# One flag on a hybrid diffusion kernel: the instruction queues ordered by the framework's second model

## Chip, core and metric

The kernel runs on one core of a Trainium2 chip. The metric is the device time of one execution in microseconds (us), lower is better. TensorE (PE) does the matmuls, VectorE (DVE) and GpSimd (POOL) the elementwise work, ScalarE (ACT) the casts and activations, SyncE (SP) issues the DMAs. Each engine works through its own queue of instructions in the order in which they stand there, and waits at an instruction until what it needs is ready.

## The reference, cut to what matters

Two layers work on 256 latent tokens and 256 context tokens of width 1024. Each layer mixes tokens with three branches (windowed GQA with a sink, multi-head latent attention, and a chunked bidirectional gated linear attention, GLA), merges them with sigmoid gates, projects, and then runs a gated FFN with a width-3 convolution.

```python
proj = (rmsnorm(x) * (1 + scale) + shift) @ w_in       # one combined projection
ya = window_gqa(q_a, k_a, v_a, ctx, sink)              # softmax attention
yb = mla(q_b, kv_b)                                    # softmax attention, low-rank q and kv
yc = gla(q_c, k_c, v_c, gates)                         # softplus gates, a scan per direction, chunks
m  = sum(sigmoid(proj_gate[b]) * (y[b] @ w_br[b]) for b in branches)
x  = x + gate1 * (m @ w_out)
u  = conv3(rmsnorm_mod(x) @ w_up) ; x = x + gate2 * (silu_gate(u) @ w_down)
```

Layer 0 needs all 512 tokens. Layer 1 puts out only the 256 latent ones. The last step is an RMS norm of the latent stream.

## The kernel before

All tensors lie transposed, 128 channels on the partitions and tokens along the row; `KT` is 8, for 1024 channels. Products are made in three parts so that they come out at nearly float32: a weight tile is loaded by SP (`raw`, L161), cast on ACT to `whi` (L164), and the rest `wlo = raw - whi` is made on DVE or POOL (L168). A `unit` (L176 on) is one output tile of 128 channels: 24 matmuls, for each of 8 channel blocks k the three products `whi` x `hh` (L172), `whi` x `hl` (L173) and `wlo` x `hh` (L174). It goes to one PSUM bank.

Each layer runs these stages in time:

- win7 (L381 to L400): the first seven output tiles, k by k. In layer 0 the modulation of channel block k+1 is worked out here too: `mods_sum` (L359) and `mods_turn` (L369) on PE, then scale and shift on ACT, then `hh`, `hl` of that block. The norms use a sum over channels (L233), a chain of ten small DVE instructions for the reciprocal root (L197 to L239), and a matmul that spreads it over the partitions (L242); DVE and ACT then make `ht`, `hh`, `hl` (L265 to L267). Layer 1 takes two passes, context and latent, so it has two norms there.
- GLA (L430 to L750): gates are `lab`, made on ACT as Exp (L546) and Ln (L549) with a table load between; DVE scans them to `bb` (L555, L557); DVE, POOL and ACT turn `bb` into factors (L593 to L601), and PE makes the products of pairs (L578). The value units (`cvr`, L473, with transposes to `cv`, L484) are work for PE that does not need the gates.
- Attention, twice four pairs of heads (L800 to L880): scores (L813, L817) to a PSUM tile, row maximum on DVE, Exp on ACT (L828) into a `p` buffer, a scale (L834), PE transposes (L850), `pth` on ACT (L854), `ptl` on DVE (L855), outputs (L866, L869). Units of the gates and branches stand between these as work for PE.
- Merge and w_out (L770 to L784, L1012 to L1029): `m` is summed over branches, `mh`, `ml` are made from it (L1012, L1013), then eight units of w_out. In layer 0 DVE also works through rows of the modulation product, `jk` (L104), one per loaded tile and stream.
- FFN (L1045 to L1146): norm, up units, convolution on ACT and DVE (L1088 to L1092), down units.

The program text is written in the order of the algorithm, with hand-made lists of work to fill in. What stands in each engine's queue is decided by the framework, which orders the instructions by a planner's model of the engines, on top of the dependences. Buffers of a pool are handed out in that order too. The context that does this is opened in one place, and it is the line that the change touches:

```python
    with tile.TileContext(nc) as tc:
        hybrid(nc, tc, aps, out)
```

## Time and profile before

| | |
|---|---|
| median of 3 runs | 1519.2 us (1518.48 to 1521.23) |
| profiled execution, its own time | 1519.25 us |
| its span, first to last instruction | 1517.5 us |
| PE busy | 1438.5 us, 95% |
| PE weight loads (PEld) busy | 1243.2 us, 82% |
| DVE busy | 1218.2 us, 80% |
| ACT, POOL busy | 811.7 us (53%), 494.6 us (33%) |
| DMA | 213.28 MB, mean 141 GB/s |
| mean granted TensorE clock | 0.981 |

The span is cut into stages below by the time at which they ran. Busy time of PE is the time in which a matmul is under way; matmuls overlap by pipelining, so the time from one start to the next is the better measure of what one costs. Idle time of PE is the stage's length less its busy time. The granted clock is 1.00 where TensorE runs at 2.4 GHz and 0.50 where it runs at 1.2 GHz.

### The profile page before, as it was taken

What the parts mean: (1) busy time and instruction counts of PE and PEld (TensorE: products, weight loads), DVE (VectorE), ACT (ScalarE), POOL (GpSimd) and SP (SyncE); (2) the same over time, 40 slices, a digit from 0 to 9 for tenths busy, and PEclk for the clock granted to TensorE, in tenths of its full rate; (3) what the DMA queues carried; (4) which work ended last, traced back from release to release, by engine and by line L of the source; (5) the groups of instructions that cost most, each with busy time, mean ns of one, the idle gap of its engine ahead of it and who ended that gap; (6) DMA issues with size and microseconds to landing.
All of it is one profiled execution on the core that took longest, in us unless ns stands there. A gap on an engine that the chain in (4) does not pass through costs nothing. (4 is left out here: it accounts for less than half of the span.)

```text
span 1517.5 us, 27758 instructions
## 1 busy us (share of the span) xinstructions
PE 1438.5 (95%) x10062; PEld 1243.2 (82%) x10062; DVE 1218.2 (80%) x2289; ACT 811.7 (53%) x1698; POOL 494.6 (33%) x407
## 2 busy tenths in 40 slices
PE   6988999999999899999999999988989899989997
PEld 4766867778788799788888889967878889989997
DVE  5688597786888979798877979978777886897886
ACT  4565355565653346534244235675466776665663
POOL 0065233233320001446544640034354443133231
PEclk9999999999999999999999999999999999999999
DMA  8411122222236575444645865532132235556553
GB/s 315 169 50 62 46 76 78 72 74 77 84 105 224 178 229 182 139 158 149 214 139 157 289 232 153 182 105 79 56 102 85 89 108 186 179 163 198 175 172 93
DMA packets 107432, 213.28 MB, mean 141 GB/s; under 512 B 12000, under 2 KB 21600, under 8 KB 106272
## 3 DMA queue, kind: packets, MB, share of 16 engines
q1 hardware_dynamic: 106608, 210.86, 42.6%
q8 instruction: 79, 1.29, 0.3%
q10 hardware_dynamic: 688, 0.66, 0.1%
q14 instruction: 57, 0.47, 0.1%
HBM read 210.42 MB, written 1.05 MB: 139 GB/s over the span
## 5 line engine op out<-in xcount | busy, mean ns | idle before, releaser
L168 POOL TENSOR_TENSOR wlo<-raw,whi 128x512 fp32r<-128x512 f32 (+1 forms) x270 | 373.8, 1390 | 711.5 <-ACT whi L164 464.0
L164 ACT CAST whi<-raw 128x512 fp32r<-128x512 f32 (+1 forms) x614 | 360.5, 597 | 320.0 <-PE ps_mm L173 136.4
L172 PE MATMUL ps_mm<-hh,whi 128*128 128x512 f32 (+1 forms) x808 | 298.3, 369 | 11.7 <-ACT cvr L473 8.5
L173 PE MATMUL ps_mm<-hl,whi 128*128 128x512 f32 (+1 forms) x808 | 292.7, 362 | 0.0
L174 PE MATMUL ps_mm<-hh,wlo 128*128 128x512 f32 (+1 forms) x808 | 292.4, 362 | 0.2 <-DVE wlo L168 0.2
L168 DVE TENSOR_TENSOR wlo<-raw,whi 128x512 fp32r<-128x512 f32 (+1 forms) x344 | 238.1, 703 | 44.0 <-ACT whi L164 39.3
L172 PEld LDWEIGHTS ps_mm<-hh,whi 128*128 128x128 f32 x808 | 155.4, 192 | 38.9 <-ACT cvr L473 8.7
L174 PEld LDWEIGHTS ps_mm<-hh,wlo 128*128 128x128 f32 x808 | 154.9, 192 | 26.0 <-DVE wlo L168 0.6
L173 PEld LDWEIGHTS ps_mm<-hl,whi 128*128 128x128 f32 x808 | 155.4, 192 | 23.8 <-issue 0.4
L104 DVE SCALAR_TENSOR_TENSOR jk<-wm,sil 128x1024 f32<-128x1024 f32 x112 | 172.8, 1543 | 1.5 <-DMA wm<-wmod 0.4
L172 PE MATMUL ps_pair<-hh,whi 128*128 128x512 f32 (+1 forms) x312 | 109.8, 353 | 2.0 <-DVE cy L1092 1.7
L174 PE MATMUL ps_pair<-hh,wlo 128*128 128x512 f32 (+1 forms) x312 | 109.0, 352 | 0.3 <-DVE wlo L168 0.2
L173 PE MATMUL ps_pair<-hl,whi 128*128 128x512 f32 (+1 forms) x312 | 109.2, 351 | 0.0
L854 ACT CAST pth<-ps_pair 128x512 fp32r<-128x512 f32 (+1 forms) x96 | 49.4, 515 | 38.7 <-PE ps_pair L850 26.9
L172 PEld LDWEIGHTS ps_pair<-hh,whi 128*128 128x128 f32 x312 | 58.5, 188 | 11.6 <-ACT whi L164 3.2
L174 PEld LDWEIGHTS ps_pair<-hh,wlo 128*128 128x128 f32 x312 | 58.4, 188 | 9.6 <-DVE wlo L168 0.7
L855 DVE TENSOR_TENSOR ptl<-ps_pair,pth 128x512 fp32r<-128x512 f32 (+1 forms) x96 | 57.4, 597 | 10.8 <-ACT pth L854 10.2
L173 PEld LDWEIGHTS ps_pair<-hl,whi 128*128 128x128 f32 x312 | 58.6, 188 | 8.7
L172 PE MATMUL ps_mm<-ach,whi 128*128 128x256 f32 (+1 forms) x200 | 63.7, 319 | 1.2 <-ACT ach L1125 0.7
L173 PE MATMUL ps_mm<-acl,whi 128*128 128x256 f32 (+1 forms) x200 | 63.5, 317 | 0.0
L174 PE MATMUL ps_mm<-ach,wlo 128*128 128x256 f32 (+1 forms) x200 | 63.4, 317 | 0.0
L174 PE MATMUL ps_mm<-mh,wlo 128*128 128x256 f32 x192 | 55.4, 289 | 4.7 <-DVE wlo L168 4.7
(673 smaller groups left out, 3582.2 us busy)
## 6 DMA issues: line engine op xcount, KB each, us to landing
raw<-wup SPq DMA_DIRECT2D x184, 256.0 KB, 3.0
raw<-win SPq DMA_DIRECT2D x182, 256.0 KB, 2.7
wm<-wmod SPq DMA_DIRECT2D x72, 512.0 KB, 3.9
raw<-wdn SPq DMA_DIRECT2D x88, 256.0 KB, 2.9
raw<-wbr SPq DMA_DIRECT2D x48, 256.0 KB, 2.6
raw<-wout SPq DMA_DIRECT2D x48, 256.0 KB, 3.0
wm<-wm SPq DMA_DIRECT2D x8, 1024.0 KB, 8.1
x<-xT SPq DMA_DIRECT2D x16, 256.0 KB, 4.8
```

The source lines that it names most:

```text
L104: V.scalar_tensor_tensor(out=jk, in0=wm, scalar=1.0, in1=sil[:, s], op0=ALU.mult, op1=ALU.mult, accum_out=MOD[l][:, s, t:t + 1])
L164: S.copy(hi[:, :ncols], raw[:, :ncols])
L168: e.tensor_tensor(out=lo[:, :ncols], in0=raw[:, :ncols], in1=hi[:, :ncols].bitcast(F32), op=ALU.subtract)
L172: mm(o, ah, bh, start=start, stop=False)
L173: mm(o, ah, bl, start=False, stop=False)
L174: mm(o, al, bh, start=False, stop=stop)
L854: S.copy(dh, tv)
L855: V.tensor_tensor(out=dl, in0=tv, in1=dh.bitcast(F32), op=ALU.subtract)
```

## The change

The context gets one keyword. The same instructions are issued with the same dependences; the framework orders them with its second model, which follows engines and queues in time.

```diff
-    with tile.TileContext(nc) as tc:
+    with tile.TileContext(nc, schedule_with_timeline_sim=True) as tc:
         hybrid(nc, tc, aps, out)
```

Each engine has as many instructions as before (PE 9060, DVE 2146, ACT 1606, POOL 405, SP 740), but many stand elsewhere: on PE by up to 125 places, on DVE up to 53, on ACT up to 29, on SP up to 19. By the time at which they ran before, PE's order is the same in the two FFNs (from 650 to 900 us, and from 1360 us on), and differs in the rest. Three places follow; the number ahead of a row is its place in the engine's queue.

The first is ACT in the GLA stage of layer 0. `lab` are the two gate tiles, `cvr` copies a value unit out of PSUM. Before:

```order
74 L543 ACTIVATE lab_709<-ps_pair_723,pp_65 128x512
75 L546 ACTIVATE lab_708<-lab_708 128x1024
76 L546 ACTIVATE lab_709<-lab_709 128x1024
77 L549 ACT_TABLE_LOAD
78 L549 ACTIVATE lab_708<-lab_708 128x1024
79 L549 ACTIVATE lab_709<-lab_709 128x1024
80 L465 ACT_TABLE_LOAD
81 L465 ACTIVATE thc_742<-ps_mm_83 128x512
82 L473 COPY cvr_745<-ps_mm_746 128x512
```

And with the change:

```order
73 L473 COPY cvr_745<-ps_mm_746 128x512
74 L543 ACTIVATE lab_709<-ps_pair_723,pp_65 128x512
75 L484 COPY cv_665<-ps_o_784 128x128
76 L543 ACTIVATE lab_708<-ps_pair_716,pp_65 128x512
77 L546 ACTIVATE lab_708<-lab_708 128x1024
78 L484 COPY cv_667<-ps_o_784 128x128
79 L164 CAST whi_1051<-raw_1049 128x512
80 L164 CAST whi_1069<-raw_1067 128x512
81 L473 COPY cvr_876<-ps_mm_877 128x512
82 L543 ACTIVATE lab_709<-ps_pair_723,pp_65 128x512
83 L465 ACTIVATE thc_742<-ps_mm_83 128x512
84 L546 ACTIVATE lab_709<-lab_709 128x1024
```

The copy `cvr_745` moved from behind the Exp, Ln and both table loads to ahead of them. The copy of the next value unit, `cvr_876`, and two casts now stand ahead of the second gate tile and of both Ln, which follow behind row 84. In layer 1 the same happens with `cvr_10658`.

The second is DVE at the end of the merge of layer 0. `ml` are the low parts of the merged rows, `wlo_5644` is the first `wlo` of w_out, whose unit is `ps_mm_5640`. Before:

```order
710 L784 TENSOR_TENSOR m7_2244<-m7_2244,gt_5561 128x512
711 L136 SCALAR_TENSOR_TENSOR ab0_69<-mod0_67,pp_65 128x8 x2
712 L138 COPY ab0_69<-mod0_67 128x8
713 L1013 SCALAR_TENSOR_TENSOR ml2_5617<-m2_2239,mh2_5616 128x512
714 L1013 SCALAR_TENSOR_TENSOR ml3_5621<-m3_2240,mh3_5620 128x512
715 L1013 SCALAR_TENSOR_TENSOR ml4_5625<-m4_2241,mh4_5624 128x512
716 L1013 SCALAR_TENSOR_TENSOR ml5_5629<-m5_2242,mh5_5628 128x512
717 L1013 SCALAR_TENSOR_TENSOR ml6_5633<-m6_2243,mh6_5632 128x512
718 L1013 SCALAR_TENSOR_TENSOR ml7_5637<-m7_2244,mh7_5636 128x512
719 L168 TENSOR_TENSOR wlo_5644<-raw_5641,whi_5643 128x512
```

And with the change:

```order
697 L782 SCALAR_TENSOR_TENSOR gt_5501<-gt_5501,ps_mm_5503 128x512
698 L168 TENSOR_TENSOR wlo_5644<-raw_5641,whi_5643 128x512
699 L104 SCALAR_TENSOR_TENSOR jk_5306,mod0_67<-wm_5302,sil_75 128x1024
700 L784 TENSOR_TENSOR m6_2243<-m6_2243,gt_5501 128x512
701 L168 TENSOR_TENSOR wlo_5662<-raw_5659,whi_5661 128x512
702 L104 SCALAR_TENSOR_TENSOR jk_5310,mod0_67<-wm_5308,sil_75 128x1024
703 L1013 SCALAR_TENSOR_TENSOR ml6_5633<-m6_2243,mh6_5632 128x512
704 L168 TENSOR_TENSOR wlo_5682<-raw_5679,whi_5681 128x512
705 L104 SCALAR_TENSOR_TENSOR jk_5312,mod0_67<-wm_5308,sil_75 128x1024
706 L782 SCALAR_TENSOR_TENSOR gt_5561<-gt_5561,ps_mm_5563 128x512
```

`wlo_5644` moved ahead of the last two merged rows, `ml1` to `ml5` are made earlier, each when its row is done, and 15 of the `jk` rows moved behind. On PE, 21 matmuls of `ps_mm_5640` and 21 of the next unit (all that needs only the rows up to `m6`) now stand ahead of the last three of each.

The third is PE in win7 of layer 1, between the pass over the context and the pass over the latent tokens. `ps_o_10125` carries the spread norm of the second pass, `hh_9881` and `hl_9882` are its first block. Before:

```order
4297 L172 MATMUL ps_pair_10084<-hh_9969,whi_10255 128x256
4298 L173 MATMUL ps_pair_10084<-hl_9970,whi_10255 128x256
4299 L242 MATMUL ps_o_10125<-dg_10142,ones_66 128x256
4300 L174 MATMUL ps_pair_10084<-hh_9969,wlo_10256 128x256
4301 L172 MATMUL ps_pair_10084<-hh_9969,whi_10255 128x256
```

And with the change:

```order
4380 L173 MATMUL ps_o_10088<-hl_10020,whi_10384 128x256
4381 L174 MATMUL ps_o_10088<-hh_10019,wlo_10385 128x256
4382 L242 MATMUL ps_o_10125<-dg_10142,ones_66 128x256
4383 L172 MATMUL ps_pair_10084<-hh_9881,whi_10411 128x256
4384 L172 MATMUL ps_pair_10085<-hh_9881,whi_10411 128x256
4385 L173 MATMUL ps_pair_10084<-hl_9882,whi_10411 128x256
4386 L174 MATMUL ps_pair_10084<-hh_9881,wlo_10412 128x256
```

The spread (L242) moved from the fifth of eight blocks of the first pass to its very end, directly ahead of the first matmul that needs what is made from it. The sums for it (L233) moved back by 105 places.

## Rows read from the trace of the kernel before

**Rows 1.** Windows by stage; columns: length, PE, PEld, DVE, ACT, POOL busy, clock, DMA, GB/s.
```profile
78.00:205.00 127.00, 114.30 (x1466) 91.72 (x1465) 100.38 (x175) 63.60 (x122) 59.38 (x59) 0.92 0.17 53
205.00:480.00 275.00, 270.25 (x1401) 219.75 (x1400) 213.35 (x444) 160.99 (x384) 79.39 (x65) 1.00 0.29 95
480.00:560.00 80.00, 74.68 (x416) 65.38 (x416) 71.10 (x130) 30.65 (x54) 0.00 (x0) 0.96 0.65 211
...
987.00:1100.00 113.00, 102.50 (x1026) 84.73 (x1024) 87.81 (x192) 64.15 (x142) 43.47 (x62) 0.92 0.23 79
1100.00:1260.00 160.00, 145.68 (x1094) 132.60 (x1093) 127.15 (x245) 108.52 (x256) 71.03 (x51) 0.99 0.31 100
```

**Rows 2.** Waits of PE, whole span: us in total, times, longest.
```profile
PE ps_mm L172 <- ACT cvr L473: 8.5, 2, 4.4
...
PE ps_mm L174 <- DVE wlo L168: 4.9, 2, 4.7
...
PE ps_mm L172 <- ACT ach L1125: 4.0, 2, 3.3
...
PE ps_pair L172 <- DVE cy L1092: 1.7, 1, 1.7
```

**Rows 3.** Timeline of ACT at the gates of layer 0: start, duration, instruction.
```profile
78.62 1.28 ACT L549 ACT_TABLE_LOAD   x1
...
83.72 0.58 ACT L473 COPY cvr<-ps_mm 128x512 f32<-128x512 f32 x1
```

**Rows 4.** Timeline of PE in the value unit of layer 0.
```profile
85.37 0.63 PE L174 MATMUL ps_mm<-hh,wlo 128*128 128x512 f32 x1
85.80 0.63 PE L172 MATMUL ps_mm<-hh,whi 128*128 128x512 f32 x1
...
90.78 0.39 PE L173 MATMUL ps_mm<-hl,whi 128*128 128x512 f32 x1
91.01 0.40 PE L174 MATMUL ps_mm<-hh,wlo 128*128 128x512 f32 x1
```

**Rows 5.** Timeline of PE at the start of w_out, layer 0.
```profile
526.37 0.28 PE L172 MATMUL ps_mm<-mh,whi 128*128 128x256 f32 x1
526.49 0.28 PE L173 MATMUL ps_mm<-ml,whi 128*128 128x256 f32 x1
...
532.59 0.58 PE L174 MATMUL ps_mm<-mh,wlo 128*128 128x256 f32 x1 [4.70 <-DVE wlo L168]
...
533.18 0.41 PE L173 MATMUL ps_mm<-ml,whi 128*128 128x256 f32 x1
533.39 0.41 PE L174 MATMUL ps_mm<-mh,wlo 128*128 128x256 f32 x1
```

**Rows 6.** Timeline of DVE ahead of that start.
```profile
523.20 1.22 DVE L104 SCALAR_TENSOR_TENSOR jk<-wm,sil 128x1024 f32<-128x1024 f32 x1
...
528.24 3.69 DVE L1013 SCALAR_TENSOR_TENSOR ml<-m,mh 128x512 fp32r<-128x512 f32 x6
```

**Rows 7.** Timeline of PE in win7 of layer 0, second block's turn and start.
```profile
22.81 0.50 PE L369 MATMUL ps_o<-cst,mrow 128*128 128x2 f32 x4
...
28.18 0.39 PE L172 MATMUL ps_pair<-hh,whi 128*128 128x512 f32 x1
```

**Rows 8.** Timeline of DVE at the second norm of layer 1.
```profile
963.17 0.16 DVE L197 TENSOR_SCALAR rv<-ps_o 128x2 f32<-128x2 f32 x1 [0.60 <-PE ps_o L233]
968.36 0.48 DVE L239 TENSOR_SCALAR dg<-cst,ry 128x128 f32<-128x128 f32 x2
...
971.00 0.48 DVE L267 SCALAR_TENSOR_TENSOR hl<-ht,ab,hh 128x256 fp32r<-128x256 f32 x1
```

**Rows 9.** Waits of PE in the attention of layer 1, 1100 to 1260 us.
```profile
PE ps_mm L172 <- DVE qf L942: 3.1, 5, 1.2
PE ps_o L869 <- DVE ptl L855: 3.1, 4, 1.6
PE ps_o L866 <- ACT pth L854: 2.9, 3, 1.6
```

## The prediction, made before the changed kernel ran

> **What bounds the kernel now.** I read the windows by stage first, since the average hides what differs between stages. In the attention of layer 0 PE is busy 270.25 of 275 us, so there is hardly anything to win there [rows 1]. PE's own idle time sits elsewhere: 12.7 us in the GLA stage of layer 0 (127 less 114.30), 5.3 us in merge and w_out of layer 0, 10.5 us in the GLA stage of layer 1 and 14.3 us in its attention [rows 1]. In those stages DVE isn't full either (100.38 of 127 us, 127.15 of 160 us), so what is late there is a chain through several engines and not one engine's throughput. Next I read what PE waited for. Three waits stand out: two for the copy `cvr` on ACT, 8.5 us together and the longer one 4.4, and one of 4.7 us for `wlo` on DVE [rows 2]. All three are a matter of order. The copy stood in ACT's queue behind the softplus of the gates: a table load of 1.28 us at 78.62, the Ln, another load, and only at 83.72 the copy of 0.58 us [rows 3]. The `wlo` stood behind rows of `jk` (1.22 us each) and behind six `ml` of 3.69 us together, none of which that matmul needs [rows 6].
>
> A long wait costs more than itself. Behind the wait at the value unit, matmuls of 512 columns start every 0.43 us (85.37 to 85.80), later in the same unit every 0.23 us (90.78 to 91.01) [rows 4]. Behind the wait at w_out they start every 0.21 us instead of 0.12 (533.18 to 533.39, 526.37 to 526.49, both 256 columns) [rows 5]. That is TensorE at 1.2 instead of 2.4 GHz; the granted clock of the two GLA stages is 0.92 for that reason [rows 1]. Some 13 matmuls of 512 columns ran so behind each `cvr` wait (13 x 0.20 = 2.6 us) and 22 of 256 columns at w_out (22 x 0.09 = 2.0 us).
>
> **The change, place by place.** No instruction is added or removed, so the sum of work per engine stays, and only waits and the clock can change. The two FFN stretches whose order is the same I put at 0. The sum is against the profiled execution, 1519.25 us, which is the median of the runs (1519.2).
>
> *w_out of layer 0.* `wlo_5644` is now ahead of most `jk` and the last `ml`, and 42 matmuls that need nothing of `m7` stand ahead of the ones that do: 42 x 0.12 = 5 us of cover for the last merged row. The wait of 4.7 and the slow clock of 2.0 go, 6.7 us. Against it: some `jk` of 1.22 us now fall among the w_out units, so DVE is a little fuller there. I take -6, bounds -7 and -3.
>
> *GLA, layer 0.* `cvr_745` goes ahead of the softplus, so the wait of 4.1 (8.5 less 4.4) and the clock's 2.6 go: -6.7 if nothing else moves. But the Ln now stands behind the copy of a second value unit, and that copy behind 24 matmuls of 0.23 us, 5.6 us. With that copy (0.6), a later head (2.2, below) and the Abs, Exp and tanh that stand behind the copy (some 3 us, five at about the copy's length), the gates are ready some 12 us later than before, an estimate. Everything on the long chain scans, factors, products starts that much later. DVE, which carries most of it, is idle 26.6 us of this stage [rows 1], partly because the factors wait for the gates; the casts, subtractions and value copies are done early now and don't stand among the factors later. I take it that DVE makes up about half, so of the 6.7 us gained some 6 are given back: -1, bounds -6.7 (all absorbed) and +8 (a third absorbed).
>
> *GLA, layer 1.* The same move. The wait is 4.4, the clock's share 2.8. The gates come some 4.5 us later here: the second unit's 5.6, less about 1 of gate work that runs meanwhile, and no late head. PE idles 10.5 us in this stage anyway [rows 1] and gets three units to fill with, earlier than before. I take -3, bounds -7.2 and +4.5.
>
> *Attention, layer 1.* From order and start-to-start intervals I count how much PE work stands between a score and the transposes that need its softmax. Of 16 steps it grows in 11 (in one from about 9 to 15 us) and shrinks in 5, in one of them by half, from about 8 to 4 us. That makes a new stall; the longest of this kind now are 1.6 us [rows 9], and I put it at 2. The waits that more work in between can cover are the three of [rows 9], 9.1 us. Two thirds of these gone and one stall new: -4, bounds -9 and +2.
>
> *Attention, layer 0.* Here the distance grows in nearly all steps too, but idle time is only 4.75 us [rows 1]. With more steps under way the four `p` buffers of this layer become short: in four places a score now stands less than 2 us of PE work behind the transposes that free the buffers which the Exp in front of it needs. I price each at a copy and a half (0.58 us [rows 3]), about 0.8 us: +3, less 1.5 of the old waits: +1.5, bounds -3 and +5.
>
> *Head, layer 0.* The turn of the second channel block ran at 22.81, behind two matmuls of the first block, and that block's own first matmul at 28.18 [rows 7]. Now it stands behind all 18 matmuls of the first block, 16 x 0.23 = 3.7 us later. The path from turn to `hh` is up to 5.4 us long [rows 7]. Before, PE's own work just covered it; now 3.7 less about 1.5 of work that stands between is uncovered: +2.2, bounds 0 and +5. Two loads of constants are also moved ahead of a weight tile on SP's queue here; they are small.
>
> *Second norm, layer 1.* The chain from the sums to the spread's input took 5.2 us (963.17 to 968.36) and from there to the first `hl` 2.6 us more (to 971.00, and its 0.48) [rows 8]. Before, 46 matmuls stood between sums and spread, and the rest of the first pass behind it. Now 23 stand between (23 x 0.12 = 2.8 us) and nothing behind the spread. 5.2 less 2.8, less a little as fewer `wlo` stand in DVE's chain: 1.8. Then 2.2 until `hl`. +4, bounds +2 and +7 (with the clock falling too).
>
> *FFN starts.* In layer 0 14 matmuls of another unit (3.3 us) stand ahead of the one that waited 1.7 us for `cy` [rows 2]: gone. In layer 1 the first four units are interleaved in four PSUM banks, so that `hh` can come later; but all four end together, and the wait of 3.3 us for the convolution behind them (the row names `ach`; the bank is freed by `cy`) [rows 2] stays and may grow by 1. With the spread there covered by 22 more matmuls: -2, bounds -4 and +2.
>
> Sum: -6 - 1 - 3 - 4 + 1.5 + 2.2 + 4 - 2 = -8.3, so 1511.
>
> **A rule that speaks against it.** In the first units of layer 1's FFN, 96 matmuls now go round four banks in groups of one to three; before, they went unit by unit. The interval there is 0.12 us as in [rows 5], and at 0.21 they would cost 96 x 0.09 = 8.6 us more, just the gain. The rows speak against that: win7 goes round seven banks before as well, and behind the turn its matmuls follow each other without a wait until the second block [rows 7]. The Trainium skill, "TensorE: Matmul & The Clock Gate", section "A second HAM failure mode: psum-queue depth-cycling", says that a kernel which cycled through PSUM banks had small idles between groups, and its clock went to and fro between the two levels. By that rule this place would run at 1.2 GHz in part; the trace doesn't bear it out for the banks that are cycled already.
>
> **Rivals.**
> 1. *The gates become the bound: slower.* In both GLA stages the product chain ends later by most of what the softplus is delayed: +8 and +4.5 in place of -1 and -3, so 16.5 more: 1527.5. For it: the delay is sure from the order, and the scans have no other source. Against it: DVE's 26.6 us of idle time in that stage. It decides from the point where the two stages together cost over 4 us more than before instead of giving 4 back, about 2 us later for each chain's last product.
> 2. *All gaps close: much faster.* The three waits and their clock go in full (-6.7, -7.2, -6.7), attention of layer 1 gives 9, and the losses stand as counted (+1.5 + 2.2 + 4 - 2): -23.9, 1495. For it: the longer distances nearly everywhere. Against it: in the GLA stages the time is a chain's, and PE's early work leaves it idle later.
> 3. *Waits only move: no change.* PE works 1438.5 us whatever the order, and each gap closed opens another within the stage: 1519, with anything from -3 to +3.
> 4. *Bank cycling slows the clock*, as above: -8.3 + 8.6, 1519.5.
>
> That the change does nothing is ruled out by the order itself.
>
> **How the numbers follow.** My forecast (1505 to 1516) has 0.45, rival 2 has 0.13, rival 3 0.13, rival 4 0.03, rival 1 0.26. A tenth on either side left out gives 1494 to 1529: the low end is rival 2, the high end rival 1 and a little. Within 0.2% (3 us, about what a measurement of this kernel can tell from no change) are rivals 3 and 4: 0.16. Faster: 0.45 + 0.13 = 0.58. Slower: 0.26.
>
> **What would show it.** Right, if no wait for `cvr` or for `wlo` at w_out is left and the windows of the GLA stages have a clock near 1.00; if the first scan of layer 0 comes about 12 us later and the stage still ends within a few us of before; and if new waits of about 2 us each show at L242 and at the first `hl` of layer 1's second pass. Wrong, if DVE is full to the end of the GLA stage and the products wait for factors (rival 1), if `p` buffers or DMA put a row of waits into the attention that isn't there now, or if a place that I put at nothing, the order of loads on SP above all, makes matmuls wait for `whi`.

## The result: slower by 3.2%

| | before | after |
|---|---|---|
| median | 1518.84 us (1517.59 to 1521.23, 4 runs) | 1566.7 us (1565.43 to 1571.53, 4 runs) |
| ratio | | 1.0319, 95% interval 1.0293 to 1.0345 |
| span of the profiled execution | 1517.5 us | 1563.6 us |
| PE busy, PE idle in the span | 1438.5, 79.0 us | 1453.7, 109.9 us |
| mean granted clock | 0.981 | 0.968 |

The same work takes 46.1 us more of span: 30.9 us of new idle time on PE, and 15.2 us in which PE is busy longer with the same matmuls. To see where, I cut the span after the change at the places in PE's queue where as much of the matmul work is done as before at the edges of [rows 1]. The windows of the changed kernel by stage:

```profile
core 0: us, PE busy (x) PEld busy (x) DVE busy (x) ACT busy (x) POOL busy (x), PEclk, DMA share, GB/s
0.00:87.00 87.00, 70.05 (x373) 51.08 (x374) 44.50 (x97) 37.85 (x80) 1.12 (x7) 0.96 0.59 212
87.00:214.30 127.30, 112.39 (x1461) 89.44 (x1459) 92.66 (x154) 62.93 (x121) 60.56 (x58) 0.95 0.18 54
214.30:518.00 303.70, 282.37 (x1404) 227.39 (x1405) 222.18 (x460) 165.40 (x389) 80.79 (x66) 0.96 0.27 82
518.00:593.80 75.80, 74.11 (x416) 64.80 (x415) 73.43 (x132) 30.80 (x54) 0.00 (x0) 0.98 0.67 207
593.80:691.30 97.50, 91.72 (x564) 81.68 (x564) 75.08 (x147) 51.51 (x93) 28.17 (x21) 0.95 0.55 175
691.30:940.30 249.00, 249.00 (x1080) 202.05 (x1079) 208.10 (x278) 90.49 (x148) 136.57 (x90) 1.00 0.60 191
940.30:1031.50 91.20, 88.09 (x633) 82.98 (x632) 81.61 (x185) 50.61 (x103) 3.07 (x4) 0.96 0.56 171
1031.50:1144.50 113.00, 98.73 (x1025) 80.88 (x1024) 86.66 (x193) 63.88 (x145) 45.56 (x62) 0.98 0.28 84
1144.50:1305.20 160.70, 146.27 (x1094) 135.97 (x1094) 125.42 (x237) 106.03 (x250) 68.56 (x50) 0.96 0.30 92
1305.20:1398.20 93.00, 85.09 (x694) 84.24 (x693) 77.57 (x167) 61.53 (x130) 20.04 (x15) 0.96 0.57 171
```

Set beside the lengths before, the head (78 us then) lost 9.0, GLA of layer 0 0.3, attention and merge of layer 0 (275) 28.7, w_out won 4.2 (80), the FFN start of layer 0 (91) lost 6.5, the norm stage of layer 1 (87) 4.2, its GLA 0.0, its attention 0.7, its FFN start (90) 3.0. The rest won 2.1: 46.1 in all. The FFN stretch from 651 to 900 us, whose order is the same, takes 249.0 us both times.

PE's waits in the changed kernel, to be read against [rows 2]:

```profile
PE ps_o L242 <- DVE dg L239: 11.5, 5, 3.5
PE ps_mm L172 <- DVE qf L942: 9.0, 4, 3.7
PE ps_pair L749 <- DVE osb L717: 9.0, 4, 4.0
PE ps_pair L578 <- DVE ex L601: 8.8, 4, 4.3
PE ps_mm L172 <- DVE cy L1092: 5.3, 1, 5.3
PE ps_pair L813 <- ACT p L828: 3.7, 3, 1.7
```

The waits for `cvr` (8.5) and for `wlo` at w_out (4.7) are gone, as forecast. In their place each row is the end of a dependent chain, or a PSUM bank that such a chain has to free (the spread of a norm, the rotated query, the scan's normalized output, a factor, the convolution, an Exp). ACT's waits say the same from the other side. First two rows before, then the same two after:

```profile
ACT whi L164 <- PE ps_mm L173: 136.4, 117, 2.2
ACT whi L164 <- PE ps_pair L173: 43.4, 37, 2.1
```

```profile
ACT whi L164 <- PE ps_mm L173: 152.1, 143, 3.3
ACT whi L164 <- PE ps_pair L173: 67.0, 51, 4.1
```

A cast of a weight tile waits until PE is done with the tile whose buffer it takes. In the second order such a cast reaches the front of ACT's queue before its buffer is free 194 times and not 154, and holds the queue 219 us and not 180. Whatever stands behind it on ACT waits too. What that costs can't be read from these rows, since nothing behind may be needed yet; the experiments below price it.

### The profile page after: what moved, and what is told of

Its sections match the earlier page's. It is cut to its first block, busy times and chain, and to the rows that moved or that the text cites. A ratio compares the mean times of both kernels' runs of the same rounds, so it can differ in the third digit from the quotient of the medians.

```text
span 1563.6 us, 27811 instructions
## 1 busy us (share of the span) xinstructions
PE 1453.7 (93%) x10062; PEld 1255.5 (80%) x10062; DVE 1208.9 (77%) x2289; ACT 816.8 (52%) x1698; POOL 490.3 (31%) x407
## 4 chain that ended last, share of the span: by engine, by line
PE 78%; DVE 14%; ACT 4%; issue 2%; POOL 1%; DMA 1%; SPq 0%; DVEq 0%; ACTq 0%; POOLq 0%
PE ps_mm L172 15%; PE ps_mm L173 15%; PE ps_mm L174 15%; PE ps_pair L172 5%; PE ps_pair L173 5%; PE ps_pair L174 5%; PE ps_pair L813 2%; PE ps_o L173 2%; PE ps_o L172 2%; PE ps_o L174 2%; DVE wlo L168 2%; PE ps_pair L850 2%; PE ps_o L869 1%; PE ps_o L866 1%; ACT whi L164 1%
## 5 line engine op out<-in xcount | busy, mean ns | idle before, releaser
L168 POOL TENSOR_TENSOR wlo<-raw,whi 128x512 fp32r<-128x512 f32 (+1 forms) x270 | 369.4, 1371 | 720.2 <-ACT whi L164 605.0
L164 ACT CAST whi<-raw 128x512 fp32r<-128x512 f32 (+2 forms) x614 | 364.6, 598 | 393.1 <-PE ps_mm L173 152.1
L168 DVE TENSOR_TENSOR wlo<-raw,whi 128x512 fp32r<-128x512 f32 (+2 forms) x344 | 237.3, 696 | 66.2 <-ACT whi L164 57.6
L172 PE MATMUL ps_mm<-mh,whi 128*128 128x256 f32 x192 | 55.1, 289 | 1.4 <-DVE x L1029 1.4
```

The costliest lines, as they stand in the source:

```text
L164: S.copy(hi[:, :ncols], raw[:, :ncols])
L168: e.tensor_tensor(out=lo[:, :ncols], in0=raw[:, :ncols], in1=hi[:, :ncols].bitcast(F32), op=ALU.subtract)
L172: mm(o, ah, bh, start=start, stop=False)
```

## The experiments

In all but the last two kernels the orders of both models are taken from the program, and each engine's queue is then pinned to one of them, or to a mixture. `PLACES` are stretches of the queues that follow the second model, the rest follows the first. `MOVES` are instructions set ahead of another one. No work changes. That pinning costs nothing is seen from the run of `cvr` (1.0004) and from `ffn0_turn` (1.0000) below, and more directly from stretches that a pinned kernel leaves in the first order: between the places in PE's queue that run at 173.4 and 400.2 us before, 226.8 us apart, head, gla0, out0 and ffn0 take 226.5 to 227.1 us. Ratios are to the kernel before on the same chip.

**Where the loss is.** Theory A: each stretch's own order costs what that stretch lost. Rival B: the loss is carried over from one early place. Rival C: it isn't the order. Six kernels take one stretch each from the second model.

```diff
+PLACES = [{'PE': (0, 258), 'Activation': (0, 77), 'DVE': (0, 94), 'Pool': (0, 3), 'SP': (0, 47)}]
...
+PLACES = [{'PE': (258, 1059), 'Activation': (77, 180), 'DVE': (94, 241), 'Pool': (3, 56), 'SP': (47, 70)}]
...
+PLACES = [{'PE': (1059, 2163), 'Activation': (180, 440), 'DVE': (241, 573), 'Pool': (56, 115), 'SP': (70, 138)}]
...
+PLACES = [{'PE': (2163, 3040), 'Activation': (440, 579), 'DVE': (573, 801), 'Pool': (115, 127), 'SP': (138, 225)}]
...
+PLACES = [{'PE': (3040, 3534), 'Activation': (579, 666), 'DVE': (801, 918), 'Pool': (127, 147), 'SP': (225, 277)}]
...
+PLACES = [{'PE': (4616, None), 'Activation': (814, None), 'DVE': (1127, None), 'Pool': (237, None), 'SP': (413, None)}]
```

Head (0 to 72 us):

> The second model's order only from the start to the end of layer 0's win7 (0 to 72 us of the kernel before), the first model's order everywhere else. Theory A (each stretch costs by itself what the two traces differ by in it): 9.0 us slower than before, 1528. Rival B (a stretch costs because of what earlier stretches leave behind: late inputs, a backlog on DVE, loads): for this one, which has nothing ahead of it, also 9, so it only tells whether the difference read off the traces is right. Rival C (the cost is not in the order of the queues but in what comes with the flag elsewhere): no change, 1519.

First scan and its products (72 to 175 us):

> The second model's order only in the GLA stage of layer 0 (72 to 175 us). Theory A: 3.4 us slower, 1522. My prediction's own value for this place was 1 us faster. Rival B: the gates come 2 to 9 us earlier here than in the changed kernel since the head is not late, so the chain is covered and it is up to 3 us faster, 1516.

State products and attention of layer 0 (175 to 401 us):

> The second model's order only from the out norm of GLA to the middle of layer 0's second attention (175 to 401 us). Theory A: 18.3 us slower, 1537. Rival B: the waits here come from branches and values that arrive late from the stages ahead, so with those on time it costs at most a third, 6 us, 1525. The prediction had 1.5 us.

Merge and w_out (401 to 567 us):

> The second model's order only from the middle of layer 0's second attention to the end of w_out (401 to 567 us). Theory A (each stretch costs by itself what the two traces differ by in it): 3.2 us slower, 1522, made of a loss of about 11 in the rest of the attention and merge and a gain of about 8 at the start of w_out. Rival B (cost carried over from earlier stretches): only the gain at w_out is left, 6 to 8 us faster, 1511.

FFN start of layer 0 (567 to 650 us):

> The second model's order only around the FFN norm and first up units of layer 0 (567 to 650 us). Theory A: 6.4 us slower, 1525.5, with PE waiting some 3.5 us for the spread of the norm (L242) and about 1 us each for the sums and the first hh. Rival B: no change, since the norm's squares come late only because w_out runs late.

Layer 1 from 900 us on:

> The second model's order only in layer 1 (900 us to the end), the first model's in all of layer 0. Theory A: 5.8 us slower, 1524, the sum of 4.2 in win7, 0 in GLA, 1.3 in attention and 0.3 in the FFN. Rival B: between no change and 6 us faster, since layer 1 then starts with nothing late.

| run | median, us | ratio, 95% interval | us more | theory A |
|---|---|---|---|---|
| head | 1527.72 | 1.0058 (1.0040 to 1.0075) | 8.8 | 9.0 |
| gla0 | 1526.19 | 1.0049 (1.0026 to 1.0072) | 7.4 | 3.4 |
| att0 | 1541.34 | 1.0145 (1.0116 to 1.0173) | 22.0 | 18.3 |
| out0 | 1525.3 | 1.0045 (1.0029 to 1.0061) | 6.8 | 3.2 |
| ffn0 | 1524.66 | 1.0040 (1.0022 to 1.0058) | 6.1 | 6.4 |
| l1 | 1528.31 | 1.0058 (1.0038 to 1.0078) | 8.8 | 5.8 |

(Us more: the ratio's excess times the base of the same chip, 1517.86 or 1518.49.) Every stretch loses by itself, so B and C fall. The six add to 59.9 us, the whole order costs 48, and four of them cost more alone than A says. Two of these can be followed in the traces. The stretch of gla0 itself takes 108.4 us alone, 104.6 in the changed kernel and 101.3 before, so behind the late head part of its loss is hidden. That of att0 takes 245.4 us alone, about as in the changed kernel (245.1, and 226.8 before), but the merge and w_out behind it, which follow the first order, take 172.2 us and not 166.7: there B holds for a small part.

**The two credits of the prediction, alone.** First order, with only the copy `cvr` of both layers set ahead of the Ln:

```diff
+MOVES = [('Activation', ['I-783'], 'I-732'),
+         ('Activation', ['I-10696'], 'I-10642')]
```

> The first model's order with one instruction moved in each layer: the copy cvr on ACT stands ahead of the Ln and its table load, not behind the second load. Nothing else moves. If PE's own work sets the end of the GLA stage, the two waits (4.1 and 4.4 us) and the slow clock behind them (2.6 and 2.8) go: 14 us faster, 1504. If the chain from the gates to the products sets it, as the prediction's rival 1 says, PE only waits later: 0 to 1 us slower, 1519, with the time back in waits for factors and in L749.

Measured: 1518.97 us, 1.0004 (0.9991 to 1.0018). No gain. PE's waits in this kernel:

```profile
PE ps_pair L578 <- DVE ex L601: 9.3, 3, 7.7
...
PE ps_o L478 <- DVE scr L466: 5.2, 1, 5.2
```

The waits for `cvr` are gone, and one of 7.7 us for the first factors and one of 5.2 us stand behind the value units in their place. In layer 0 PE did its value unit earlier and then waited for the gates' chain, whose scans start at 82.3 us as before (82.2). In layer 1 it waited for `scr`, which stands on DVE behind the scans. The slow clock moved too: from 84.5 to 90 us it was 0.50 before and is 0.91 now, from 90 to 110 us it was 1.00 and is 0.77. Then w_out, with the order of DVE alone changed (`wlo_5644`, `wlo_5662` and five `ml` ahead; nine instructions, `jk` and what is summed from them, behind):

```diff
+MOVES = [('DVE', ['I-5397', 'I-5461', 'I-5586', 'I-5463', 'I-5587', 'I-5589', 'I-5588', 'I-5590', 'I-5591'], 'I-5722'),
+         ('DVE', ['I-5646'], 'I-5615'),
+         ('DVE', ['I-5619', 'I-5623', 'I-5627', 'I-5631', 'I-5635'], 'I-5582'),
+         ('DVE', ['I-5664'], 'I-5639')]
```

> The first model's order with DVE alone changed at the end of layer 0's merge: wlo_5644, wlo_5662 and the ml ahead of the last three jk and what sums them, which go behind the fourth wlo of w_out. If the prediction's step for this place is right, the wait of 4.7 us and the slow clock of 2.0 go and nothing else is late: 6.5 us faster, 1512.5. If DVE is what bounds w_out, the jk come back as waits for wlo there: no change.

Measured: 1516.11 us, 0.9979 (0.9966 to 0.9992). This credit is real, some 3 us alone, and this version beats both kernels; in its trace the merge and w_out take 164.2 us and not 166.7. PE's wait there is now

```profile
PE ps_mm L172 <- DVE x L1029: 2.9, 1, 2.9
```

since the `jk` that were moved behind must still run before `x` can be made: the last of them ends at 532.6 us, `x` starts at 533.69, and DVE is busy 16.1 of the 17 us from 520 to 537.

**Repairs of one link.** Four kernels take a losing stretch and set one late thing ahead: `kl`, `q` behind `osb` on DVE; the second half of each copy of the transposed `p` (`pth`, `ptl`) right behind the first, ten times; the gates' second half and Ln ahead of `cvr_876` and two casts; the squares and sums of the FFN's norm.

```diff
+MOVES = [('DVE', ['I-2179', 'I-2182', 'I-2214', 'I-2216'], 'I-2377')]
...
+MOVES = [('Activation', ['I-3358'], 'I-3303'),
...
+MOVES = [('Activation', ['I-728', 'I-743', 'I-731', 'I-732', 'I-733'], 'I-1053')]
...
+MOVES = [('Activation', ['I-6345', 'I-6348', 'I-6351', 'I-6354', 'I-6357'], 'I-6465'),
...
```

> The second model's order from 175 to 401 us, as in att0, with four instructions moved on DVE: the two kl (L744) and two q (L729) that stand among the small steps of the GLA norm go behind its four osb (L717). If the loss at L749 comes from work put into that chain, osb is ready 3 us earlier, the wait of 3.5 us there and part of the slow clock behind it (0.72 for 10 us, 2.8 us) go: 4 to 6 us less than att0, 1536. If the chain is late for another reason (the copies on ACT, PE's own work ahead of it), within 1 us of att0, 1541.

> As att0, but in ten attention steps (transposes 3347 to 4193) the second pth of a step stands right behind the first on ACT and the second ptl right behind the first on DVE, as they nearly did in the first model's order, with nothing put between them. If the loss in the second half of this stretch comes from other ready work put ahead of what an output needs next, the waits for ptl of 3.05 and 2.27 us and their clock go: 5 to 9 us less than att0, 1534. If it comes from too few p buffers (the two waits of L813 for p, 1.6 and 1.75 us), these stay and at most 3 us is won, 1539.

> The second model's order in the GLA stage of layer 0, as in gla0, with ACT's second gate tile, both Exp and Ln (and the tanh among them) moved ahead of the casts and the cvr copy that wait for the second value unit. If the late gates are what costs (the prediction's rival 1), the 7.4 us of gla0 go, to within 1 us of before, 1519. If the order of DVE and POOL behind the gates costs as well, 3 us or more stay, 1522.

> The second model's order from 567 to 650 us, as in ffn0, with the sums of the norm made early: its five squares on ACT ahead of the cast of whi_6463, the additions on DVE ahead of wlo_6464, and the four L233 on PE 48 matmuls earlier. L242 stays where it is. If the cost is that nothing covers the chain between sums and spread, the wait of 4.9 us there and 1.1 behind it go: 0 to 1 us slower than before, 1519.5. If the wlo that are now 2.5 us later on DVE are needed by then, PE waits for those: 1522 or more.

| run | median, us | ratio, 95% interval | what PE waits for now |
|---|---|---|---|
| att0_osb | 1541.95 | 1.0160 (1.0139 to 1.0181) | at L749 5.9 us for `scr` in place of 3.5 for `osb` |
| att0_sib | 1555.65 | 1.0253 (1.0229 to 1.0277) | at L813 11.5 us for `p` in place of 3.7 |
| gla0_ln | 1527.19 | 1.0052 (1.0027 to 1.0077) | 5.9 us for `cvr`; the Ln ends at 90.6 as in gla0 (90.7) |
| ffn0_sum | 1525.88 | 1.0061 (1.0046 to 1.0076) | at L242 5.2 us for `dg`, 4.9 in ffn0 |

None gives anything back, and att0_sib costs some 16 us more than att0. In each, waits of 5 us or more stand at the same link or at another.

**The whole chain of a stretch.** Read side by side, the traces showed why. In ffn0 the ten steps of the reciprocal root stand on DVE behind three `wlo` whose casts wait for a load. ACT first, then DVE:

```profile
593.65 1.27 ACT L164 CAST whi<-raw 128x512 fp32r<-128x512 f32 x2 [3.29 <-DMA raw<-wup]
...
594.30 2.17 DVE L168 TENSOR_TENSOR wlo<-raw,whi 128x512 fp32r<-128x512 f32 x3 [1.76 <-ACT whi L164]
596.39 0.15 DVE L197 TENSOR_SCALAR rv<-ps_o 128x2 f32<-128x2 f32 x1
...
598.15 0.48 DVE L239 TENSOR_SCALAR dg<-cst,ry 128x128 f32<-128x128 f32 x2
```

The sums were ready at 593.8, yet the chain starts at 596.39. In the head, the turn of a later block (L369) stands on PE behind the matmuls of the block ahead. Its input `mrow` is there at 48.73 us, the turn runs at 52.47, and ACT's scale (L371) waits for it. A cast ahead of the scale was stopped for 4.05 us, but the casts are done at 52.85, just ahead of the turn, so it would be the next late link and isn't the one that ends last. DVE, PE, ACT:

```profile
48.31 0.42 DVE L361 COPY mrow<-ps_o 128x256 f32<-128x256 f32 x1 [0.39 <-PE ps_o L359]
...
52.47 0.51 PE L369 MATMUL ps_o<-cst,mrow 128*128 128x2 f32 x4
...
51.51 0.62 ACT L164 CAST whi<-raw 128x512 fp32r<-128x512 f32 x1 [4.05 <-PE ps_pair L173]
...
53.02 0.35 ACT L371 ACTIVATE ab<-ps_o,c,pp 128x2 f32<-128x2 f32 x1 [0.17 <-PE ps_o L369]
```

In gla0 two of the four gate matmuls stand behind a value unit on PE and the last behind two (71.2, 77.0, 77.6 and 83.9 us; before, 71.8 to 75.2), and the Ln on ACT behind the casts of the next ones:

```profile
76.98 0.62 ACT L164 CAST whi<-raw 128x512 fp32r<-128x512 f32 x1 [2.18 <-PE ps_mm L173]
...
83.81 0.62 ACT L164 CAST whi<-raw 128x512 fp32r<-128x512 f32 x1 [2.18 <-PE ps_mm L173]
...
84.81 0.69 ACT L543 ACTIVATE lab<-ps_pair,pp 128x512 f32<-128x512 f32 x1
...
89.63 1.07 ACT L549 ACTIVATE lab<-lab 128x1024 f32<-128x1024 f32 x1
```

Theory D: the chain stands behind fill on engines that work in order, and all its links have to be pulled ahead together. Rival E: the fill was spent too early and nothing is left to lie beside the chain. Four kernels keep a stretch's second order and pull the chain ahead on PE, ACT and DVE; a few of the moves:

```diff
+         ('DVE', ['I-6413', 'I-6414', 'I-6415', 'I-6416', 'I-6417', 'I-6418', 'I-6419', 'I-6420', 'I-6421', 'I-6423', 'I-6424'], 'I-6545'),
...
+         ('Activation', ['I-6500', 'I-6504', 'I-6508'], 'I-6645'),
+         ('PE', ['I-6479'], 'I-6546')]
...
+MOVES = [('PE', ['I-328', 'I-329'], 'I-341'),
...
+         ('Activation', ['I-444', 'I-445', 'I-450', 'I-453'], 'I-545'),
...
+MOVES = [('PE', ['I-724'], 'I-753'),
...
+         ('Activation', ['I-728', 'I-730', 'I-731', 'I-732', 'I-733'], 'I-976'),
...
+         ('PE', ['I-3596', 'I-3597', 'I-3598', 'I-3599'], 'I-3723'),
...
```

> The second order in 567 to 650 us alone, as in ffn0 (1524.7 us, +6), but with the squares and sums of the norm, the ten steps of its rsqrt (L197 to L239) ahead of wlo_6543 on VectorE, the spread L242 ahead of the unit 6542 on TensorE, and the first three normed tiles (L265, L266, L267) ahead of the casts 6643 and 6644, which wait until TensorE frees a tile. Theory D: the wait of 4.9 us at L242 goes, 1518 to 1521 us. Rival E: a wait of 3 us or more stays there, 1523 us or more.

> The second order in 0 to 72 us alone, as in head (1527.7 us, +8.9), but with the turns of the modulation pulled ahead: on TensorE the small matmuls L359 and L369 of three blocks ahead of the fill unit that they stood behind, on ScalarE and VectorE L371, L372, L265, L266, L267 and L361 of these blocks ahead of the casts L164 and L168 that wait for TensorE to free a tile. Theory D (the chain stands behind the fill): 1519 to 1522 us, the gates L541 at 72 to 74 us and not at 77.2. Rival E (the fill has been spent early): 1525 us or more, the waits only move.

> The second order in 72 to 175 us alone, as in gla0 (1526.2 us, +7.4), but with the gates pulled ahead on three engines: the matmuls L541 of ps_pair_723 and of both second halves ahead of the fill units 746 and 877 on TensorE, L543, L546 and L549 ahead of the casts 956 and 974 on ScalarE, L544, L553, L555 and L557 ahead of the casts 957, 975, 1052 and 1070 on VectorE. Theory D: the Ln ends near 82 us (90.7 in gla0, 81.9 before), bb_712 near 83.5, the last factor at 157 to 159 and not at 162.4, 1519 to 1522 us. Rival E: the scan's end and the time stay as in gla0, 1525 us or more.

> The second order in 175 to 401 us alone, as in att0 (1541.3 us, +22), but with 14 groups of the transposes L850 of p pulled ahead on TensorE, each ahead of the scores L813 of two steps later, so that the p buffers (four, two to a step) come free before the exps L828 that need them; six copies of the transposed p that would close a circle go ahead with them. Theory D: the exps no longer start right at the end of the transposes of two steps before, the waits of L813 for p (1.6 and 1.8 us) go, and 8 to 16 us come back: 1525 to 1533 us. Rival E (no fill is left to lie beside the steps): 1538 us or more. Rival F (ScalarE or the one bank of the transposes is the ring, not the buffers): 1538 us or more too, with longer waits at L850 itself.

| run | median, us | ratio, 95% interval | stretch without the moves |
|---|---|---|---|
| ffn0_turn | 1517.22 | 1.0000 (0.9987 to 1.0013) | 1.0040 |
| head_turn | 1524.81 | 1.0041 (1.0020 to 1.0062) | 1.0058 |
| gla0_gate | 1523.8 | 1.0036 (1.0018 to 1.0054) | 1.0049 |
| att0_tr | 1576.17 | 1.0379 (1.0354 to 1.0405) | 1.0145 |

*FFN start: D holds.* All 6 us came back, with the fill still in the second order's place elsewhere. The sums alone, pulled ahead in ffn0_sum, gave nothing back; the ten steps there still start at 596.81 us, in ffn0_turn at 589.35. The wait at the spread in ffn0 and in ffn0_turn:

```profile
PE ps_o L242 <- DVE dg L239: 4.9, 1, 4.9
```

```profile
PE ps_o L242 <- DVE dg L239: 0.2, 1, 0.2
```

*Head and first scan: in part.* About 2.6 and 2.0 us came back of 8.8 and 7.4. Both times lie between what D wanted (up to 1522) and what E wanted (1525 or more), and the intervals overlap with those without the moves. The traces say how far the moves reached. In head_turn the first gate matmul runs at 74.6 us, at 77.2 in head, at 71.8 before. The turns of three later blocks came early, and that of the second block, which I had not moved, still runs at 27.2 us (22.8 before). In gla0_gate the Ln ends at 83.7 (90.7 in gla0, 81.9 before), but the scan starts at 87.0 (90.8 in gla0, 82.2 before), behind a `wlo` on DVE that waited 4.80 us for its cast, and DVE's first factor is still done only at 103.1 (103.2 in gla0), since links that I had not moved stand behind the same kind of cast. PE no longer waits for the factors (6.5 us in gla0), but again for `cvr`, 3.9 us. DVE and ACT in gla0_gate:

```profile
84.28 0.69 DVE L168 TENSOR_TENSOR wlo<-raw,whi 128x512 fp32r<-128x512 f32 x1 [4.80 <-ACT whi L164]
...
82.70 1.04 ACT L549 ACTIVATE lab<-lab 128x1024 f32<-128x1024 f32 x1
...
89.20 0.62 ACT L164 CAST whi<-raw 128x512 fp32r<-128x512 f32 x1 [3.67 <-PE ps_mm L173]
92.00 0.62 ACT L164 CAST whi<-raw 128x512 fp32r<-128x512 f32 x1 [2.18 <-PE ps_mm L173]
...
96.75 0.63 ACT L600 ACTIVATE ex<-ex 128x512 f32<-128x512 f32 x1
```

That supports D for this place, and doesn't prove it: the factors were not pulled ahead in a run.

*Attention: D's version of it fell.* Pulling the transposes ahead cost 35 us more. They then wait for the copy that empties their one PSUM tile:

```profile
PE ps_pair L850 <- DVE ptl L855: 27.8, 11, 5.4
```

Longer waits at L850 are what rival F had forecast. That doesn't prove it, since only six copies were pulled ahead with the 14 groups of transposes. In att0 the waits of the same steps were 3.7 us for `p`, 3.5 for `ptl` at L869 and 2.3 for `ptl` at L850. In att0 an Exp starts when the transposes of two steps before have run (p_3661 at 350.0 us, these from 349.6 to 349.9; p_3732 at 358.1, these from 357.7 to 358.1), so the `p` buffers looked like the ring. Layer 0 has four, layer 1, which lost 0.7 us, has six. The last two kernels give layer 1 four as well, in either order:

```diff
-                pts = [common.tile([128, 512], F32, tag="p", name="p", bufs=(4, 6)[l])[:, :w] for _ in range(2)]
+                pts = [common.tile([128, 512], F32, tag="p", name="p", bufs=(4, 4)[l])[:, :w] for _ in range(2)]
```

> The kernel before (first order) with four p buffers in layer 1 in place of six, as layer 0 has. Theory G (the buffers decide, but only when the transposes come late): 1518 to 1526 us, since in the first order the transposes follow within some 4 us of the exps. Rival H (something else in layer 0): the same, 1518 to 1526 us; this run is the base of the next one.

> The changed kernel (second order) with four p buffers in layer 1 in place of six. Theory G: the gap to the first order with four buffers grows from 48 to 60 us or more, the attention of layer 1 (1141 to 1306 us in the changed kernel) gets waits of TensorE for p at the scores L813. Rival H: the gap stays at 42 to 54 us, that stretch keeps its time within 4 us of what the first order with four buffers shows there.

Measured: 1516.7 us in the first order, 1.0001 (0.9986 to 1.0016), and 1566.69 us in the second, 1.0321 (1.0285 to 1.0357). The gap is 50 us by the medians, 48.5 by the ratios, as it was. By line and tile name, the queues of PE, ACT and DVE hold the same order as with six buffers, so only the buffers differ. Layer 1's attention shows no wait for `p`; its longest sum from 1140 to 1310 us is the same row that it has with six buffers:

```profile
PE ps_mm L172 <- DVE qf L942: 9.0, 4, 3.7
```

So the number of buffers does not decide in layer 1. Six buffers in layer 0, the direct trial, were not run. In att0's own stretch PE is idle 17.9 us (6.4 before) and busy 7.2 us longer with the same matmuls; the idle time is spread over waits at L749 (5.8 us), L813 (4.0), L869 (3.5) and shorter ones, none above 3.5. Which link is the first late one in the attention of layer 0 stays open.

## Why the prediction was wrong

The sign was wrong: 1511 forecast, 1566.7 measured, and far above the range. Rival 1 had the right sign and 8 us. Two of the text's own signs of being wrong showed: products that wait for factors (L578 for `ex`, 1.9 us before and 8.8 after) and waits for `p`. Of the 54 us between the sum (-8.3) and the span (+46.1), 27 lie in the attention and merge of layer 0, 11.5 in the FFN starts and 6.8 in the head. Step by step, with the stage differences above:

- *w_out: right.* -6 forecast with bounds -7 and -3; the stage shows -4.2, and DVE's reordering alone -3.
- *Second norm of layer 1: right in kind.* +4 forecast, +4.2 measured, with the two waits that the text wanted, but 1.7 us at L242 and 1.1 at the first `hh` in place of 1.8 and 2.2. PE's idle time grew by 2.2 us and its busy time by 2.0, at a clock of 0.96 and not 1.00; the +4 had counted idle time alone.
- *GLA, layer 0: the sum right by luck, the credit wrong.* -1 forecast, +0.3 measured; between places where the same matmuls have run in both orders (72.1 to 173.4 us before, 81.1 to 185.7 after) it is +3.3, and alone the stretch costs 7.4, close to the +8 of rival 1. The scan starts 18 us later where the text had 12, 9 of them from the head (the rows are below). The stage made up most of what the head had not caused. But the -6.7 for the removed wait was never there: the run of `cvr` alone gave nothing, because the gates' chain, and not PE's queue, set the stage's end. "PE idles while it waits" was read as "PE's wait costs". With the copy ahead, the same idle time is found at L578. Nor was the stage's clock of 0.92 due to these waits alone: without them, from 72 to 173.4 us, it is 0.92 in the run of `cvr` as before.
- *GLA, layer 1:* -3 forecast, 0.0 measured, by the same step. The clock did rise, from 0.92 to 0.98, and PE's busy time fell by 3.8 us; its idle time grew by as much.
- *Head: mis-sized.* +2.2 forecast, bounds 0 and +5; +9.0 measured, 8.8 alone. I followed one turn, that of the second block, and it came 3.8 us later (26.65 us, 22.81 before), as forecast. The same pattern came back at three later blocks, where the turn stands on PE behind the matmuls of the block ahead: from the start of the sums (L359) to the turn it takes 5.3 us there, 2.5 to 3.2 before.
- *FFN starts: wrong sign.* -2 forecast; +6.5 and +3.0 measured. I counted the wait for `cy` in layer 0 as gone and gave the spread in layer 1 a cover. I did not look where the ten small DVE steps ahead of the spread of layer 0 stood against the `wlo` of the unit behind. The 3.5 us at L242 in the waits above are that place. In layer 1 the wait for `cy` grew from 3.3 for the convolution to 5.3, which the text had put at "may grow by 1", and the interleaved units waited 2.1 us for `xel`.
- *Attention of layer 1:* -4 forecast, +0.7 measured, inside the bounds. Of the three waits of [rows 9] those for `ptl` (3.1 us) went and those for `pth` fell from 2.9 to 1.7, as the text wanted; the one for `qf` grew from 3.1 to 9.0.
- *Attention of layer 0 and merge: the step that decided, a term mis-sized.* +1.5 forecast with bounds -3 and +5; +28.7 measured. The stage was taken as full (270.25 of 275 us [rows 1]), so I looked only for short stalls at the `p` buffers. There are such stalls (three at L813, 3.7 us together, the row for `p` above), but the stage lost 8.9 us in the merge alone, to waits of 2.2 and 2.3 us for `vb` and `ybh`, and 19.8 us before it. A full stage has nothing to win and everything to lose; its bounds should have been the widest.

The first scan of layer 0, before and then after:

```profile
82.21 1.22 DVE L555 TENSOR_TENSOR_SCAN bb<-smask,mn 128x512 f32<-128x512 f32 x1
```

```profile
100.44 1.22 DVE L555 TENSOR_TENSOR_SCAN bb<-smask,mn 128x512 f32<-128x512 f32 x1
```

Behind these steps stands one error. I priced the waits that the new order removes from measured rows, and the waits that it adds only at the places where I looked. The trace of before has rows for the first kind only. An order that had few waits is better evidence for its own places than I gave it: of the changes in PE's, ACT's and DVE's queues I followed some ten, and each of the six stretches lost.

Rival 4, that cycling through four banks slows the clock, can be read directly. After the change layer 1's FFN goes round four banks from 1368.7 to 1383.6 us. Early in it PE waits 2.14 us for `xel`, until 1371.60. Granted clock (the last but two of the columns) from there on:

```profile
1372.00:1375.00 3.00, 3.00 (x16) 3.00 (x16) 3.00 (x9) 1.65 (x4) 0.00 (x0) 0.52 0.32 87
1375.00:1383.60 8.60, 8.60 (x78) 8.60 (x76) 8.24 (x21) 5.94 (x12) 0.00 (x0) 1.00 0.32 104
```

Behind the wait the clock is 0.52 for 3 us, then 1.00 while the matmuls go on round the same four banks, one every 0.11 us. So the cycling didn't keep the clock down, and the rival falls: some 16 matmuls ran slowly, behind a wait, and not 96. The Trainium skill, "TensorE: Matmul & The Clock Gate", section "A second HAM failure mode: psum-queue depth-cycling", speaks of small idles between the groups; PE is busy all of the 8.60 us at 1.00, so the case doesn't contradict it.

## What to carry to other kernels

When a change reorders a tuned kernel, price the waits that it can add as carefully as those that it removes: for each chain (norm, gates, turn, softmax) look up what stands ahead of each link on each in-order engine, and above all whether a cast or copy there waits for a buffer. Taking away a wait of the busiest engine gains nothing if a chain that ends later is waited for next; the run that removes that wait alone tells. If a scheduler's order loses, it can be pinned stretch by stretch: here one stretch of it was repaired entirely, and one reordering taken alone made the best version, at 0.9979 (0.9966 to 0.9992).

## What the runs showed of the hardware

Idle time of PE cost more than its length here: 46.1 us for 30.9 us of it in the whole kernel, 1.5 times, and 1.8 times in the merge. There the same matmuls took 75.00 us without any idle time before; after the change 4.98 us of idle time came in and the stretch grew by 8.9 us, since PE's busy time grew by 3.92 us too. Windows of that stretch, before and then after:

```profile
405.00:480.00 75.00, 75.00 (x385) 62.71 (x385) 60.34 (x116) 41.03 (x92) 13.96 (x11) 1.00 0.43 140
```

```profile
434.10:518.00 83.90, 78.92 (x390) 64.95 (x389) 57.77 (x113) 42.94 (x97) 14.47 (x11) 0.96 0.35 113
```

Its mean granted clock is 0.96 and not 1.00, so part of it ran at 1.2 GHz. In the 20 us from 223 us on, in which the wait of 3.54 us at L749 ends (224.96), the mean granted clock was 0.74:

```profile
223.00:243.00 20.00, 15.77 (x58) 11.06 (x59) 16.79 (x26) 6.79 (x15) 8.02 (x6) 0.74 0.24 66
```

The prediction had such a factor for the waits that it removed (6.7 us for one of 4.1 and for one of 4.7, 1.6 and 1.4 times), and for those added only in one bound.
